# S5 weights stored without the other group's zeros, with one store a tile, two rotation buffers, and the first input transfers issued back to back

## The chip, the cores and the metric

The kernel is one program on one NeuronCore of a Trainium2 chip. Its time is the device time of one execution in microseconds. Five engines run their own instruction streams in order and wait for each other through semaphores: PE (TensorE, matmuls), ACT (ScalarE), DVE (VectorE), POOL (GpSimd) and SP (SyncE, which here only issues transfers). ACT issues transfers too.

## The reference

A sequence of 256 tokens of width 1024 goes through eleven stages: feed-forward blocks and four mixers. Only the first stage (a gated feed-forward block, `ffn0`) and the second (the S5 mixer) are touched. S5 is a linear recurrence in 64 groups with 64 complex states each:

```python
u = h @ w_in                                   # 256 x 1024, 16 channels a group
mag = exp(a_re * dt)
lam_re, lam_im = mag * cos(a_im * dt), mag * sin(a_im * dt)
bb_re, bb_im = cmul(coef_re, coef_im, b_re, b_im)
# for each step t: state = lam * state + bb u_t (complex, by group)
#                  y_t   = Re(c state) + d_skip u_t
g = gelu(y)
g = g * sigmoid(g @ w_glu)
return g @ w_out
```

What depends on the parameters alone (powers of lam, products with b and c) can be worked out before u is there.

## The kernel before

**Order of the work.** The program is recorded as a list of operations with engine, estimated cost and class, and then a list scheduler in the file (`Schedule`) plays it through on its own cost estimates and fixes each engine's order. At run time that order is kept: an instruction that is not ready holds up everything behind it on its engine. Class HEAD goes first, CRIT is the main path, FILL and LATE are weight matmuls, and BACK (the S5 preparation) only takes what the other classes leave. The landing of a transfer is put at `o.lat` = 2.0 us after its issue. All instructions carry the one source line of the emitter, L519, in the profile, so tiles name the work.

**Weights.** Every weight matrix is read in slabs of 512 KB (`raw`), and split into a rounded part by ACT (`whi`) and a rest by DVE (`wlo`); PE multiplies both. Six `raw`, six `whi` and five `wlo` buffers let loads and splits run ahead of PE.

**Head.** `record` puts on ACT's queue, in this order: the gains, the first of eight feature tiles of x (h, k = 0), a one-element activation `tab` that pulls in the activation table, then x's tile 1 and tiles 2 and 3 (`load_x`). Tiles 4 to 7 go on SP's queue between the weights. PE runs ten matmuls on the identity first (`warm`). The first real product needs the split of x's first tile (`xs`) and of the first weight piece.

**S5 preparation** (`s5_prep`, class BACK, during `ffn0`). After small vectors it makes, for the halves of the state dimension (`table(half)`), a table of rotations in the tile `tb` by doubling, and stores it in four pieces. There is one `tb`: the second half starts with two POOL memsets into it, and later `bt` (the b matrix) is loaded into the same tile. Then for each of eight tiles m: `enter(m)` makes `et` from `bt` and a reloaded vector `lb`, four DVE operations and four ACT copies, two for each group mask; `powers(m)` makes `gz`, three DVE operations and two ACT copies; ACT lays b out in `bz`; PE multiplies gz and bz; the product gets d added and is copied by ACT to `lag`. `et` and `gz` hold two groups side by side, and where a row belongs to one group the other group's half is zero. Each of the three goes by its own store from ACT's queue into `s5_dr[m]` (2688 elements a row with the table), from double buffers: `ets[m % 2]`, `gzs[m % 2]`, `lags[m % 2]`.

**S5 stage** (`s5`). `load(m)` reads a whole row block back into `mt` (four buffers, two of them in `ffn0`'s released `hid`; the other two in a pool that opens when all of the preparation has ended, last store included). The profile calls those in the released room `hid`. `state(m)` multiplies `et` with u, DVE runs a chain of products and a scan with the table, `outy(m)` multiplies `gz` and the lags, ACT applies gelu, and `glu(m)` and the projections follow. The first tile waits for `r_bc`, which goes through POOL (`r_col`).

Of the kernel before, what the change touches and what calls it, by code (L numbers as in the profile page):

```python
# [21 lines left out]
P = 128  # L22
T = 256
# [8 lines left out]
MT = 2688  # L32
# [142 lines left out]
class Recorder:  # L175
# [71 lines left out]
    def add(self, calls, cls):  # L247
# [5 lines left out]
        o.lat = 2.0 if o.dma else 0.0  # L253
# [270 lines left out]
class Net:  # L524
# [351 lines left out]
    def s5_prep(self):  # L876
# [9 lines left out]
        self.s5_dn = keep("s5_dn", [P, KD])  # L886
        self.s5_dr = [self.sb(f"s5_dr{m}", [P, MT], pool="dram") for m in range(KD)]
# [111 lines left out]
        tb = tmp("tb", [P, 2, 16, 64])  # L999
# [43 lines left out]
        mask = tmp("mask", [P, 2])  # L1043
        D.dma_start(out=mask, in_=A["s5_mask"])
        bt = tb.rearrange("p r j c -> p (r j c)")[:, 0:1024].rearrange("p (m r c) -> p m r c", m=KD, r=2)
# [9 lines left out]
        for z in gzs + [bz]:  # L1055
            G.memset(z, 0.0)

        def table(half):

            j0 = 16 * half  # L1060
            G.memset(tb[:, 0, :, 31:32], 1.0)
            G.memset(tb[:, 1, :, 31:32], 0.0)
            w = 1
            while w < 32:
                ew = e4[w.bit_length()]
                sh = [P, 2, 16, w]
                a4, b4 = (z[:, 0:32 * w].rearrange("p (r j c) -> p r j c", r=2, j=16) for z in (tA, tB))
                src = tb[:, :, :, 31:31 + w]
                ph = lambda i: ew[:, i, j0:j0 + 16].unsqueeze(1).unsqueeze(3).to_broadcast(sh)
                tt(V, a4, src, ph(0), MUL)  # L1070
                tt(V, b4, src, ph(1), MUL)
                tt(V, tb[:, 0, :, 31 + w:31 + 2 * w], a4[:, 0], b4[:, 1], SUB)
                tt(V, tb[:, 1, :, 31 + w:31 + 2 * w], a4[:, 1], b4[:, 0], ADD)
                w *= 2
            S.activation(tb[:, :, :, 63], e4[6][:, :, j0:j0 + 16], AF.Copy)
            for r in range(2):
                S.activation(tb[:, r, :, 0:31], tb[:, r, :, 62:31:-1], AF.Copy, scale=(1.0, -1.0)[r])
            for m in range(4):
                D.dma_start(out=self.s5_dr[4 * half + m][:, 2176:MT].rearrange("p (r j c) -> p r j c", r=2, j=4),
                            in_=tb[:, :, 4 * m:4 * m + 4, :])  # L1080
# [11 lines left out]
        def enter(m):  # L1092
# [6 lines left out]
            tt(V, a[:, 0], a[:, 0], b[:, 1], SUB)  # L1099
            tt(V, a[:, 1], a[:, 1], b[:, 0], ADD)  # L1100
            et = ets[m % 2]
            for g in range(2):
                for r in range(2):
                    S.activation(et[:, :, r, 64 * g:64 * g + 64], a[:, r], AF.Copy, scale=mask[:, g:g + 1])
            S.dma_start(out=self.s5_dr[m][:, 0:1024], in_=et.rearrange("p s r q -> p (s r q)"))

        def powers(m):
# [4 lines left out]
            gz = gzs[m % 2]  # L1112
# [4 lines left out]
            tt(V, pa, pa, pq, SUB)  # L1117
            for g in range(2):
                ps = slice(64 * g, 64 * g + 64)
                S.activation(gz[ps].rearrange("p r s j (g n) -> p (r s j) g n", g=2)[:, :, g, :],  # L1120
                             pa[ps].rearrange("p q j n -> p (q j) n"), AF.Copy)

        def tile_mats(m):
# [5 lines left out]
            gz = gzs[m % 2]  # L1129
            S.dma_start(out=self.s5_dr[m][:, 1024:2048], in_=gz.rearrange("p r s j q -> p (r s j q)"))  # L1130
            p = self.ps(5)
            with self.r.group(CRIT):
                for ri in range(2):
                    for j in range(4):
                        PE.matmul(p[32 * j:32 * j + 32, 0:P], lhsT=bz[:, ri, j, :], rhs=gz[:, ri, :, j, :], start=(ri == 0), stop=(ri == 1),
                                  skip_group_check=True)
            V.scalar_tensor_tensor(p[:, 0:32], i4, self.s5_dn[:, m:m + 1], p[:, 0:32], op0=MUL, op1=ADD)
            S.activation(lags[m % 2], p[:, 0:P], AF.Copy)
            S.dma_start(out=self.s5_dr[m][:, 2048:2176], in_=lags[m % 2])
# [10 lines left out]
    def s5(self, ph, nxt):  # L1150
# [7 lines left out]
        def share(shape):  # L1158
# [5 lines left out]
            names = "abc"[:len(shape)]  # L1164
# [10 lines left out]
        for t in zss + m4s:  # L1175
            G.memset(t, 0.0)
# [8 lines left out]

        def scale(m):
# [4 lines left out]
        def state(m):  # L1191
            u, mt = us[m], mts[m]
            et = mt[:, 0:1024].rearrange("p (s r q) -> p s r q", s=4, r=2)
            ps = [self.ps(b)[:, 0:P].rearrange("p (r c) -> p r c", r=2) for b in sbanks]
            with self.r.group(CRIT):
                for ri in range(2):
                    for s in range(4):
                        for j in range(4):
                            a = slice(32 * j, 32 * j + 32)
                            PE.matmul(ps[j][:, ri, :], lhsT=et[a, s, ri, :], rhs=u[a, s, :], start=s == 0, stop=s == 3,  # L1200
# [3 lines left out]
            tab = mt[:, 2176:MT].rearrange("p (e j c) -> p e j c", e=2, j=4)  # L1204
# [10 lines left out]
            for ri in range(2):  # L1215
# [3 lines left out]
                            mt[:, 2176:MT].rearrange("p (e q) -> p e q", e=2).unsqueeze(2).to_broadcast([P, 2, 2, T]), op=MUL)  # L1219
# [5 lines left out]
        def outy(m):  # L1225
            z, u, mt = zss[m % NZ], us[m], mts[m]
            gz = mt[:, 1024:2048].rearrange("p (r s j q) -> p r s j q", r=2, s=4, j=4)
            ps = self.ps(4)[:, 0:T].rearrange("p (s c) -> p s c", s=4)
            with self.r.group(CRIT):
                for d in range(4):  # L1230
                    for j in range(4):
                        a = slice(32 * j, 32 * j + 32)
                        PE.matmul(ps[a, d:4, :], lhsT=mt[a, 2048 + 32 * d:2080 + 32 * d], rhs=u[a, 0:4 - d, :], start=d == 0, stop=False,
# [56 lines left out]
        for m in range(KD):  # L1290
            if m < 4:
                umm(m + 4)
            state(m)
# [689 lines left out]
```

## Time and profile before

| | |
|---|---|
| median of 3 runs | 1579.7 us (1579.31 to 1580.79) |
| the profiled execution, its own time | 1576.88 us |
| its span, first to last instruction | 1575.1 us |
| PE busy | 1538.8 us, 98% |
| DVE busy | 1177.5 us, 75% |
| ACT busy | 946.3 us, 60% |

PE is busy nearly all the time, so what the change can move is PE's idle time, the time PE runs at half clock, and PE's own work for the preparation. Times in the trace count from the first instruction; 1.8 us of the execution lie outside the span.

### The profile page before, as it was taken

What the parts mean: (1) busy time and instruction counts of PE and PEld (TensorE: products, weight loads), DVE (VectorE), ACT (ScalarE), POOL (GpSimd) and SP (SyncE); (2) the same over time, 40 slices, a digit from 0 to 9 for tenths busy, and PEclk for the clock granted to TensorE, in tenths of its full rate; (3) what the DMA queues carried; (4) which work ended last, traced back from release to release, by engine and by line L of the source; (5) the groups of instructions that cost most, each with busy time, mean ns of one, the idle gap of its engine ahead of it and who ended that gap; (6) DMA issues with size and microseconds to landing.
All of it is one profiled execution on the core that took longest, in us unless ns stands there. A gap on an engine that the chain in (4) does not pass through costs nothing.

```text
span 1575.1 us, 28813 instructions
## 1 busy us (share of the span) xinstructions
PE 1538.8 (98%) x11018; PEld 1383.7 (88%) x11018; DVE 1177.5 (75%) x2205; ACT 946.3 (60%) x1800; POOL 76.2 (5%) x111
## 2 busy tenths in 40 slices
PE   8998998999999999999999999999999999999998
PEld 8998887998888888889998888989888888888887
DVE  5997878877777777767878777797876557787663
ACT  6566662466655566645666665565787447688642
POOL 1000000000000000003310000010000002100000
PEclk8999999999999999999999999999999999999999
DMA  7667887356656555655447666632665542356561
GB/s 255 216 195 266 255 307 275 133 187 189 187 185 189 184 185 188 187 163 164 134 161 226 188 186 188 207 116 90 217 203 187 188 143 78 122 178 211 186 189 40
DMA packets 94682, 289.29 MB, mean 184 GB/s; under 512 B 18768, under 2 KB 23760, under 8 KB 93520
## 3 DMA queue, kind: packets, MB, share of 16 engines
q1 hardware_dynamic: 90224, 277.44, 55.6%
q10 hardware_dynamic: 4320, 10.01, 1.7%
q8 instruction: 86, 1.41, 0.4%
q14 instruction: 52, 0.43, 0.1%
HBM read 275.22 MB, written 12.19 MB: 182 GB/s over the span
## 4 chain that ended last, share of the span: by engine, by line
PE 86%; DVE 4%; DMA 4%; issue 2%; ACT 2%; POOL 2%; SPq 1%; ACTq 0%; DVEq 0%; POOLq 0%
PE ps L519 86%; DVE wlo L519 1%; DMA s_dr<-tb 1%; DMA raw<-w_s5i 1%; DMA raw<-w_ffn 1%; POOL rs L519 1%; ACT whi L519 1%; SPq L519 1%; DVE h L519 0%; DMA tb<-s_bt 0%; DMA h<-x 0%; DMA tab<-ab_tab 0%; DVE tA L519 0%; POOL qk L519 0%; DMA pb<-s_l 0%
## 5 line engine op out<-in xcount | busy, mean ns | idle before, releaser
L519 ACT ACTIVATE whi<-raw 128x1024 fp32r<-128x1024 f32 (+3 forms) x520 | 522.8, 1011 | 417.4 <-PE ps L519 324.6
L519 PE MATMUL ps<-xs,whi 128*128 128x512 f32 (+1 forms) x2592 | 737.3, 354 | 11.6 <-ACT xs L519 8.4
L519 DVE TENSOR_TENSOR wlo<-raw,whi 128x1024 fp32r<-128x1024 f32 (+3 forms) x520 | 604.4, 1165 | 192.3 <-PE ps L519 145.2
L519 PE MATMUL ps<-xs,wlo 128*128 128x256 f32 x2080 | 567.7, 282 | 0.0
L519 PEld LDWEIGHTS ps<-xs,whi 128*128 128x128 f32 x2592 | 448.5, 190 | 75.6 <-ACT xs L519 9.1
L519 PE MATMUL ps<-hid,whi 128*128 128x512 f32 (+1 forms) x1248 | 424.0, 388 | 0.0
L519 PEld LDWEIGHTS ps<-xs,wlo 128*128 128x128 f32 x2080 | 394.6, 190 | 10.8
L519 PE MATMUL ps<-hid,wlo 128*128 128x256 f32 x1216 | 332.2, 279 | 0.0
L519 PEld LDWEIGHTS ps<-hid,whi 128*128 128x128 f32 x1248 | 229.0, 187 | 49.2 <-issue 0.4
L519 PEld LDWEIGHTS ps<-hid,wlo 128*128 128x128 f32 x1216 | 228.2, 188 | 4.3
L519 PE MATMUL ps<-whi,xs 128*128 128x256 f32 (+1 forms) x544 | 125.6, 312 | 0.0
L519 PEld LDWEIGHTS ps<-whi,xs 128*128 128x128 f32 x544 | 92.1, 188 | 1.0 <-issue 0.8
L519 PE MATMUL ps<-wlo,xs 128*128 128x256 f32 (+1 forms) x272 | 83.3, 306 | 0.0
L519 PE MATMUL ps<-oT,whi 128*128 128x256 f32 x384 | 69.7, 283 | 0.0
L519 POOL TENSOR_TENSOR r_col<-ms,mhalf 128x2 f32<-128x2 f32 x11 | 11.2, 1021 | 1207.2 <-DVE ms L519 1207.2
L519 DVE TENSOR_TENSOR hid<-hv,hid 128x256 fp32r<-128x256 f32 x88 | 37.1, 424 | 31.1 <-ACT hid L519 31.0
L519 PEld LDWEIGHTS ps<-oT,whi 128*128 128x128 f32 x384 | 58.3, 188 | 1.6 <-issue 1.2
L519 ACT ACTIVATE hid<-hv 128x256 fp32r<-128x256 f32 x88 | 36.2, 413 | 33.1 <-DVE hv L519 32.3
L519 ACT ACTIVATE zr<-zr 128x256 f32<-128x256 f32 x128 | 51.0, 410 | 7.4 <-DVE zr L519 7.4
L519 PE MATMUL ps<-oT,wlo 128*128 128x256 f32 x192 | 53.7, 280 | 0.6 <-DVE wlo L519 0.6
L519 PEld LDWEIGHTS ps<-wlo,xs 128*128 128x128 f32 x272 | 51.2, 188 | 0.1
L519 DVE TENSOR_TENSOR zr<-ps,zr 128x256 f32<-128x256 f32 x64 | 26.7, 422 | 28.0 <-ACT zr L519 27.9
(254 smaller groups left out, 1553.4 us busy)
## 6 DMA issues: line engine op xcount, KB each, us to landing
raw<-w_ffn SPq DMA_DIRECT2D x260, 512.0 KB, 4.1
raw<-w_mlp SPq DMA_DIRECT2D x128, 512.0 KB, 4.3
raw<-w_moba_q SPq DMA_DIRECT2D x32, 384.0 KB, 3.0
raw<-w_ab_in SPq DMA_DIRECT2D x18, 512.0 KB, 4.4
hid<-s_dr SPq DMA_DIRECT2D x4, 1344.0 KB, 8.9
mt<-s_dr SPq DMA_DIRECT2D x4, 1344.0 KB, 6.4
s_dr<-gz ACTq DMA_DIRECT2D x8, 512.0 KB, 6.5
s_dr<-et ACTq DMA_DIRECT2D x8, 512.0 KB, 5.8
```

Source lines behind the costliest of these rows:

```text
L519: getattr(getattr(nc, ename), method)(*[real(x) for x in a], **{n: real(x) for n, x in k.items()})
```

## The change

- The preparation keeps `et` and `gz` without the zeros: 512 elements each instead of 1024. With the lags (128) they lie in one tile `outs[m % 2]` of 1152 elements, and one store a tile goes from ACT's queue, after the lags. A row block with the table has 1664 elements instead of 2688.
- The product of gz and bz has 64 columns instead of 128; the group mask goes into two copies to the lags.
- `tb` becomes `tbs`, one tile for each half. `bt` is loaded into the first.
- In the S5 stage a new `spread(m)` puts the zeros back: two masked ACT copies into `ets[m % 2]` and two into `gzs[m % 2]`, before `state(m)`. Their zeros are set once by POOL.
- The scheduler takes 5.0 us instead of 2.0 for the landing of the preparation's transfers.
- The one-element activation between the first transfers goes; the three x transfers of ACT's queue follow each other.

```diff
-MT = 2688
+MT = 1664
...
-        o.lat = 2.0 if o.dma else 0.0
+        o.lat = (5.0 if cls == BACK else 2.0) if o.dma else 0.0
...
-        tb = tmp("tb", [P, 2, 16, 64])
+        tbs = [tmp(f"tb{i}", [P, 2, 16, 64]) for i in range(2)]
...
-        bt = tb.rearrange(...)
+        bt = tbs[0].rearrange(...)
-        gzs = [tmp(f"gz{i}", [P, 2, 4, 4, 32]) for i in range(2)]
-        ets = [tmp(f"et{i}", [P, 4, 2, P]) for i in range(2)]
-        lags = [tmp(f"lag{i}", [P, P]) for i in range(2)]
+        outs = [tmp(f"out{i}", [P, 1152]) for i in range(2)]
...
-        for z in gzs + [bz]:
-            G.memset(z, 0.0)
+        G.tensor_tensor(i4[:, 0:16], i4[:, 0:16], i4[:, 16:32], op=ADD)
+        G.memset(bz, 0.0)
...
+            tb = tbs[half]
             G.memset(tb[:, 0, :, 31:32], 1.0)
...
-            tt(V, a[:, 0], a[:, 0], b[:, 1], SUB)
-            tt(V, a[:, 1], a[:, 1], b[:, 0], ADD)
-            et = ets[m % 2]
-            for g in range(2):
-                for r in range(2):
-                    S.activation(et[:, :, r, 64 * g:64 * g + 64], a[:, r], AF.Copy, scale=mask[:, g:g + 1])
-            S.dma_start(out=self.s5_dr[m][:, 0:1024], in_=et.rearrange("p s r q -> p (s r q)"))
+            e = outs[m % 2][:, 0:512].rearrange("p (r s c) -> p r s c", r=2, s=4)
+            tt(V, e[:, 0], a[:, 0], b[:, 1], SUB)
+            tt(V, e[:, 1], a[:, 1], b[:, 0], ADD)
...
-            tt(V, pa, pa, pq, SUB)
-            for g in range(2):
-                ps = slice(64 * g, 64 * g + 64)
-                S.activation(gz[ps]..., pa[ps]..., AF.Copy)
+            tt(V, outs[m % 2][:, 512:1024].rearrange(...), pa, pq, SUB)
...
-            S.dma_start(out=self.s5_dr[m][:, 1024:2048], in_=gz.rearrange("p r s j q -> p (r s j q)"))
...
-                        PE.matmul(p[32 * j:32 * j + 32, 0:P], lhsT=bz[:, ri, j, :], rhs=gz[:, ri, :, j, :], ...)
+                        PE.matmul(p[32 * j:32 * j + 32, 0:64], lhsT=bz[:, ri, j, :], rhs=gz[:, ri, :, j, :], ...)
...
-            S.activation(lags[m % 2], p[:, 0:P], AF.Copy)
-            S.dma_start(out=self.s5_dr[m][:, 2048:2176], in_=lags[m % 2])
+            for g in range(2):
+                S.activation(o[:, 1024:1152]...[:, :, g, :], p[:, 0:64]..., AF.Copy, scale=mask[:, g:g + 1])
+            S.dma_start(out=self.s5_dr[m][:, 0:1152], in_=o)
...
+        ets, gzs = two("et", (2, 4, P)), two("gz", (2, 4, 4, 32))
-        for t in zss + m4s:
+        for t in zss + m4s + gzs:
             G.memset(t, 0.0)
...
+        def spread(m):
+            mt, et, gz = mts[m], ets[m % 2], gzs[m % 2]
+            for g in range(2):
+                S.activation(et[:, :, :, 64 * g:64 * g + 64]..., mt[:, 0:512]..., AF.Copy, scale=self.s5_mask[:, g:g + 1])
+            for g in range(2):
+                ps = slice(64 * g, 64 * g + 64)
+                S.activation(gz[ps]...[:, :, g, :], mt[ps, 512:1024]..., AF.Copy)
...
+            spread(m)
             state(m)
             outy(m)
...
-            self.load_x(0, 1, "S")
-            self.table(AF.Copy, self.ident)
-            for k in (1, 2):
-                self.load_x(k, 2 * k, "S")
+            for k in (0, 1, 2):
+                self.load_x(k, max(k + 1, 2 * k), "S")
```

## Rows read from the trace of the kernel before

**Rows 1.** Waits of PE, whole span: total us, times, longest us
```profile
PE ps L519 <- ACT xs L519: 8.4, 3, 4.6
PE ps L519 <- ACT gz L519: 6.9, 3, 5.4
```

**Rows 2.** Timeline from 0 to 20 us: start, length, what [idle before, releaser]
```profile
1.36 4.53 PE L519 MATMUL ps<-ident 128*128 128x128 f32 x20 [1.36 <-POOL ones L588]
...
1.66 1.28 ACT L519 ACT_TABLE_LOAD   x1 [1.66 <-PEq L1965]
...
2.96 0.20 ACT L519 ACTIVATE tab<-ident 128x1 f32<-128x1 f32 x1
...
7.87 1.38 ACTq L519 DMA_DIRECT2D h<-x  x2
9.29 0.72 ACT L519 ACTIVATE whi<-raw 128x256 fp32r<-128x256 f32 x2 [6.13 <-DMA raw<-w_ffn]
...
10.46 1.10 PE L519 MATMUL ps<-xs,whi 128*128 128x256 f32 x2 [4.57 <-ACT xs L519]
...
14.40 1.10 PE L519 MATMUL ps<-xs,whi 128*128 128x256 f32 x2 [0.71 <-ACT xs L519]
```

**Rows 3.** Chain that ended last, 0 to 20 us: start, length, what
```profile
3.07 4.78 DMA raw<-w_ffn
...
7.87 5.95 DMA h<-x
```

**Rows 4.** Windows of 1 us on PE: length, busy (count), granted clock, DMA share, GB/s
```profile
18.00:19.00 1.00, 1.00 (x7) 0.50 0.75 303
19.00:20.00 1.00, 1.00 (x9) 0.84 0.75 102
```

**Rows 5.** Chain that ended last, 118 to 150 us
```profile
127.94 7.96 DMA s_dr<-tb
```

**Rows 6.** Waits of DVE, 128 to 228 us
```profile
DVE tA L519 <- POOL tb L519: 6.3, 1, 6.3
...
DVE tA L519 <- DMA tb<-s_bt: 3.2, 1, 3.2
```

**Rows 7.** Windows of 2 us: length, PE, PEld, DVE, ACT, POOL, granted clock, DMA share, GB/s
```profile
146.00:148.00 2.00, 2.00 (x21) 1.58 (x22) 2.00 (x6) 1.66 (x4) 0.00 (x0) 0.50 0.95 166
148.00:150.00 2.00, 2.00 (x15) 2.00 (x15) 1.92 (x6) 0.60 (x2) 0.00 (x0) 0.74 1.01 397
...
226.00:228.00 2.00, 0.44 (x1) 0.29 (x1) 1.76 (x5) 1.58 (x5) 0.00 (x0) 0.88 0.97 346
228.00:230.00 2.00, 2.00 (x10) 1.92 (x10) 0.81 (x3) 1.27 (x3) 0.00 (x0) 0.50 1.02 422
...
234.00:236.00 2.00, 2.00 (x17) 2.00 (x17) 0.31 (x2) 0.39 (x1) 0.00 (x0) 0.91 0.23 95
```

**Rows 8.** Chain that ended last, 196 to 300 us
```profile
225.50 1.14 DVE wlo L519
...
227.56 21.55 PE ps L519 x322
```

**Rows 9.** Timeline of ACT, 219 to 231 us
```profile
228.65 0.33 ACTq L519 DMA_DIRECT2D s_dr<-et  x1
```

**Rows 10.** Timeline of PE, 95 to 160 and 248.5 to 253 us
```profile
99.00 0.64 PE L519 MATMUL ps<-gz,bz 128*32 128x128 f32 x16
...
249.18 2.09 PE L519 MATMUL ps<-hid,mt 32*128 32x64 f32 x64
```

**Rows 11.** Groups of ACT by form, 0 to 240 us: busy, mean ns | idle before
```profile
L519 ACT ACTIVATE gz<-pg 64x512 f32<-64x512 f32 x16 | 10.0, 625 | 0.9 <-DMA s_dr<-tb 0.5 <-DVE pg L519 0.3
```

**Rows 12.** Windows of the preparation and of the S5 stage (columns as rows 7)
```profile
128.00:228.00 100.00, 90.67 (x619) 80.53 (x617) 78.84 (x146) 64.69 (x118) 1.68 (x6) 0.98 0.84 276
237.00:301.00 64.00, 59.01 (x1450) 53.31 (x1451) 55.97 (x109) 16.01 (x29) 0.00 (x0) 0.95 0.59 222
```

**Rows 13.** DMA issues, 100 to 240 us: count, KB each, median us to landing
```profile
s_dr<-gz ACTq DMA_DIRECT2D x7, 512.0 KB, 6.5
```

More of the change, by code (lines that the diff above doesn't have):

```diff
@@ L1078, in table @@
             for m in range(4):
-                D.dma_start(out=self.s5_dr[4 * half + m][:, 2176:MT].rearrange("p (r j c) -> p r j c", r=2, j=4),
+                D.dma_start(out=self.s5_dr[4 * half + m][:, 1152:MT].rearrange("p (r j c) -> p r j c", r=2, j=4),
                             in_=tb[:, :, 4 * m:4 * m + 4, :])
@@ L1116, in powers @@
             tt(V, pq, by(1), rows(0), MUL)
-            tt(V, pa, pa, pq, SUB)
-            for g in range(2):
-                ps = slice(64 * g, 64 * g + 64)
-                S.activation(gz[ps].rearrange("p r s j (g n) -> p (r s j) g n", g=2)[:, :, g, :],
-                             pa[ps].rearrange("p q j n -> p (q j) n"), AF.Copy)
+            tt(V, outs[m % 2][:, 512:1024].rearrange("p (q j n) -> p q j n", q=8, j=4), pa, pq, SUB)
         def tile_mats(m):
@@ L1128, in tile_mats @@
                 S.activation(bz[ps, :, :, g * NN:(g + 1) * NN], bb[ps, :, 4 * m:4 * m + 4, :], AF.Copy)
-            gz = gzs[m % 2]
-            S.dma_start(out=self.s5_dr[m][:, 1024:2048], in_=gz.rearrange("p r s j q -> p (r s j q)"))
+            o = outs[m % 2]
+            gz = o[:, 512:1024].rearrange("p (r s j n) -> p r s j n", r=2, s=4, j=4)
             p = self.ps(5)
@@ L1134, in tile_mats @@
                     for j in range(4):
-                        PE.matmul(p[32 * j:32 * j + 32, 0:P], lhsT=bz[:, ri, j, :], rhs=gz[:, ri, :, j, :], start=(ri == 0), stop=(ri == 1),
+                        PE.matmul(p[32 * j:32 * j + 32, 0:64], lhsT=bz[:, ri, j, :], rhs=gz[:, ri, :, j, :], start=(ri == 0), stop=(ri == 1),
                                   skip_group_check=True)
-            V.scalar_tensor_tensor(p[:, 0:32], i4, self.s5_dn[:, m:m + 1], p[:, 0:32], op0=MUL, op1=ADD)
-            S.activation(lags[m % 2], p[:, 0:P], AF.Copy)
-            S.dma_start(out=self.s5_dr[m][:, 2048:2176], in_=lags[m % 2])
+            V.scalar_tensor_tensor(p[:, 0:16], i4[:, 0:16], self.s5_dn[:, m:m + 1], p[:, 0:16], op0=MUL, op1=ADD)
+            for g in range(2):
+                S.activation(o[:, 1024:1152].rearrange("p (d g n) -> p d g n", d=4, g=2)[:, :, g, :],
+                             p[:, 0:64].rearrange("p (d n) -> p d n", d=4), AF.Copy, scale=mask[:, g:g + 1])
+            S.dma_start(out=self.s5_dr[m][:, 0:1152], in_=o)
         for half in range(2):
@@ L1163, in share @@
             v = room[:, used[0] - n:used[0]].bitcast(F32)
-            names = "abc"[:len(shape)]
+            names = "abde"[:len(shape)]
             return v.rearrange(f"p ({' '.join(names)}) -> p {' '.join(names)}", **dict(zip(names, shape)))
@@ L1199, in state @@
                             a = slice(32 * j, 32 * j + 32)
-                            PE.matmul(ps[j][:, ri, :], lhsT=et[a, s, ri, :], rhs=u[a, s, :], start=s == 0, stop=s == 3,
+                            PE.matmul(ps[j][:, ri, :], lhsT=et[a, ri, s, :], rhs=u[a, s, :], start=s == 0, stop=s == 3,
                                       skip_group_check=True)
@@ L1203, in state @@
             S.activation(m4[:, :, 1:64], self.s5_m4[:, 4 * m:4 * m + 4].unsqueeze(2).to_broadcast([P, 4, 63]), AF.Copy)
-            tab = mt[:, 2176:MT].rearrange("p (e j c) -> p e j c", e=2, j=4)
+            tab = mt[:, 1152:MT].rearrange("p (e j c) -> p e j c", e=2, j=4)
             sh = [P, 2, 2, 64]
@@ L1232, in outy @@
                         a = slice(32 * j, 32 * j + 32)
-                        PE.matmul(ps[a, d:4, :], lhsT=mt[a, 2048 + 32 * d:2080 + 32 * d], rhs=u[a, 0:4 - d, :], start=d == 0, stop=False,
+                        PE.matmul(ps[a, d:4, :], lhsT=mt[a, 1024 + 32 * d:1056 + 32 * d], rhs=u[a, 0:4 - d, :], start=d == 0, stop=False,
                                   skip_group_check=True)
```

15 lines of the change are left out of this document (9 added, 6 removed).

## The prediction

> **What bounds the kernel now.** First the waits of PE over the whole span. PE is the engine that ends last, and its real idle time is small; the three longest single waits lie where this change works. Waits on `xs` come to 8.4 us in three places and waits on `gz` to 6.9 us in three, 5.4 of them in one [rows 1]. The timeline of the head places two waits on `xs`: 4.57 us before 10.46 and 0.71 before 14.40 [rows 2]; what is left of the 8.4, 3.1 us, is the one before 227.56, where S5 begins [rows 8]. Then the windows, for a cost that no idle time shows: after each of the three long waits PE runs at a granted clock of 0.50, that is 1.2 GHz, for some microseconds [rows 4, 7]. The S5 stage itself is crowded: in 64 us PE is busy 59 and DVE 56, but ACT only 16 [rows 12].
>
> So each term is a wait of PE that goes or comes, plus half of the time at half clock behind it.
>
> **Head, term A.** ACT's queue issues x's tiles 1 to 3 only at 7.87, and the chain puts the landing of a weight transfer issued at 3.07 (3.07 + 4.78 = 7.85) right ahead of it [rows 3]. The data of the two have nothing in common. What they can share is the bookkeeping of transfers in program order: with the table load (1.28) and `tab` between them, the x transfers count as later than the weights. ACT's first `whi` stands behind them in its queue and starts at 9.29, PE's first product at 10.46 [rows 2]. With `tab` gone the two issues follow x's tile 0. ACT is free of its first issues by 1.66; the two others take at most 1.38 together, which gives 3.04. The table load is not saved, only moved behind them (1.28, 4.32), and from the first `whi` to the first product it is 10.46 - 9.29 = 1.17, hence 5.49. PE's warm-up matmuls end at 1.36 + 4.53 = 5.89 [rows 2]; they now decide. Should x's tile 0 take the 5.95 of rows 3 from 1.66, the start would be near 8. I take 5.89, since it is issued when few transfers are under way.
>
> The Trainium skill (ScalarE: Activation LUTs, What ACT_TABLE_LOAD costs) speaks against a part of this: a switch costs about 2.66 us, 1.28 for the load and 1.38 for a drain. Here the load takes 1.28 and `tab` starts at 2.96, 0.02 after its end [rows 2]; the trace shows no drain. By the page the first product would come near 6.9 and term A would be about 0.5 us smaller.
>
> Idle time removed: 4.57 + 0.71 = 5.28. The clock is at half until about 19.3 (0.50, then 0.84 in the window 19 to 20 [rows 4]), 8.8 us after the first product. If it rises at that same time, half of the idle time comes back: 2.6. If it rises 8.8 us after the new start, at 14.7: before, by 19.3, PE had done (8.8 - 0.7) / 2 = 4.05 us of full-speed work; after, 4.4 + 4.6 = 9.0, a gain of 4.9. If the warm-up counts, 8.8 us from 1.36 is 10.2, and by 19.3 PE has done 2.2 + 9.1 = 11.3: a gain of 7.2. I take the middle, **-4.9** (-2.1, with the late start, to -7.2).
>
> **Rotation buffers, term B.** The store of the first half's table is issued at 127.94 and lands 7.96 later [rows 5]. The second half's memsets into the same `tb` wait for that on POOL; DVE stands 6.3 us behind them [rows 6], with the operations of `gz` and the weight splits queued behind. ACT's `gz` is late in turn, and PE, in order, stands 5.4 us at a product of gz and bz [rows 1]. Then the clock: 0.50 in 146 to 148, 0.74 in 148 to 150 [rows 7], so 2 + 1.04 us at half, a loss of 1.5. With two tiles the memsets wait for nothing. DVE's next stall, 3.2 us on `bt` loaded into the same tile [rows 6], goes too: the first tile is free once the first half's stores have landed. **-6.9**; with the other waits on gz gone as well (6.9 - 5.4 = 1.5) -8.4; and 0 if another wait takes its place.
>
> **Out buffers, a new wait.** Before, `gz` of six tiles could be made while `et` waited for `bt`. Now both go into `outs[m % 2]`, and tile m + 2 writes there only after the store of m has landed: 6.5 us for the nearest row [rows 13], while the scheduler now counts 5.0. Where it places DVE's write as early as it may, DVE stands some 1.5 us, with `wlo` behind it; five `wlo` buffers hide such a stall, but PE's in-order product of that tile doesn't. Six tiles can wait. Below, nothing; above, one full wait of the kind in term B less its clock, 5.4. I take **+1.5**, the 1.5 of the one short landing.
>
> **S5's start, term C.** PE stops at 227.56 - 3.1 = 224.5; the preparation's last store is issued at 228.65 [rows 9], and its DVE and ACT work stands between the pieces of the last `h` and `xs`; the chain also shows a `wlo` there, 1.14 [rows 8]. PE idles 3.1 us and then runs at half clock: 0.88 in 226 to 228, 0.50 in 228 to 234, 0.91 in 234 to 236 [rows 7], together 6.8 us, a loss of 3.4. If the preparation ends earlier, all of it except the `wlo` can go: 3.1 + 3.4 - 1.1 = 5.4. DVE's work in the preparation stays the same in number and size, and in 128 to 228 it is busy 79 of 100 us [rows 12]. It gets 6.3 + 3.2 = 9.5 us of stall back, but PE comes 6.9 earlier too, so it ends some 3 us earlier against PE, where 228.65 - 224.5 = 4.2 at least would be needed. Half: **-2.7** (0 to -5.4).
>
> **Narrower product, term D.** Eight products of gz and bz stand in PE's queue, 0.64 us for 16 records of 128 columns [rows 10]. The nearest row with 64 columns is S5's `state`, 2.09 us for 64 records, so 0.52 for 16 [rows 10]. 8 x 0.12 = **-1.0**; between nothing and half, -2.6.
>
> The Trainium skill (TensorE: Matmul & The Clock Gate, Wait — 56ns, not 53.3ns?) says that starts of matmuls never come closer than about 25 ns, however few the columns. Rows 10 give 33 ns a record, which agrees. By the page 16 records would take at least 0.40 and the term would end at -1.9.
>
> **The S5 stage, term E.** `spread` puts four ACT copies of 512 columns into each of eight tiles; at 0.625 us for the like [rows 11] that is 2.5 us a tile and 20 us in all. ACT is busy 16 of 64 us there [rows 12], and the loads run ahead of `state`, so the cover is ACT's idle time. If none of it covered, +20. On the other side each row block is 1664 / 2688 = 62% as long in both directions. POOL's memset of the second `gz` waits for the last store of the preparation, and `r_col` stands behind it; with that store issued before PE stops this is hidden. I take **0** (-3 to +10, half uncovered). ACT's work taken out of the preparation (six copies and two stores a tile) was off PE's path. `i4`'s add and the memsets moved out of the head run on POOL, 1.7 us busy in 100 [rows 12]: nothing.
>
> **Sum.** -4.9 - 6.9 + 1.5 - 2.7 - 1.0 + 0 = -14.0 us. The profiled execution took 1576.88, so a profile after would read 1562.9; that execution lies 2.8 us under the median of the runs, so the median goes from 1579.7 to **1565.7**.
>
> **Rivals.**
> - *The head doesn't change*: the x transfers still stand behind weight landings. For it: the trace names no reason for that order. Against: nothing but the table load and `tab` stood between. -9.1: 1570.6.
> - *DVE sets the pace*: in 128 to 228 it has 21 us of idle time [rows 12], and A and B take 12 of PE's time out of the same work; then C gives nothing and a wait of 2 more comes in: -9.3, about 1570.4.
> - *ACT in the S5 stage*: half of `spread` falls in the path, +10: 1575.7. Against it stand the 16 of 64 us.
> - *The ring of two out buffers, slower than before*: a store of the preparation lands late in the way that tb's did, and PE stands at the tile's product 5.4 us and loses 1.5 of clock. One such wait costs 6.9 where I set 1.5; without that 1.5 the gains are 15.5, so from the third of the six possible ones the kernel is slower: 1579.7 - 15.5 + 20.7 = 1584.9. For it: 6.5 against the 5.0 of the scheduler, and every tile passes it. Against: each is short by 1.5 us, not by 6.
> - *More than forecast*: clock early in A, C and D whole, B with both short waits: -7.2 - 8.4 - 5.4 - 2.6 = -23.6, 1556.1.
>
> **How the numbers follow.** Forecast 0.53, head unchanged 0.10, DVE 0.12, ACT 0.10, ring 0.08, more 0.07. No change means within 0.2%, 3.2 us, about what a measurement of this kernel can tell. Slower: 0.08 of the ring and 0.01 of ACT. Same: 0.04 of ACT, 0.03 of the forecast's edge, 0.01 of DVE. The rest is faster, 0.83. The likeliest case alone reaches from 1560 to 1571. The range goes up to 1577, past the centre of the ACT case, and down to 1557: the ring, the upper quarter of ACT, the upper case and a few hundredths of the forecast's edge are left out, 0.2.
>
> **What would show it.** A: in the timeline PE's first product on `xs` near 5.9, x's transfers issued before 3. B: no wait of PE on gz over 1 us near 140, DVE without a wait on POOL's `tb`. C: the wait before S5 under 1.5 us, no window at 0.50 behind it, the last store of the preparation before PE stops. D: products of gz and bz at 0.52. E: the stretch from the first `state` to the last glu no longer than before. The prediction is wrong if PE waits at several products of gz and bz, or on `spread` in S5.

## The result, and the profile after

| | before | after |
|---|---|---|
| median of the runs (4 each, same chip) | 1579.51 us | 1559.38 us |
| ratio, 95% interval | | 0.9874 (0.9857 to 0.9891) |
| profiled execution, its span | 1575.1 us | 1556.6 us |

The kernel is 20.1 us faster; 14.0 were forecast, and 1557 to 1577 was the range. The sum hides that its terms are off on both sides: two of them went another way than forecast, and these partly cancel. Where the two traces part is read from five landmarks on PE, each found in both traces by counting the same instructions:

| landmark on PE | before, us | after, us | gained so far | since the last |
|---|---|---|---|---|
| 64th product on `xs` | 22.89 | 16.84 | 6.05 | 6.05 (head) |
| first down product of `ffn0` | 153.63 | 136.56 | 17.07 | 11.0 (preparation) |
| last down product of `ffn0` | 217.69 | 200.29 | 17.40 | 0.3 |
| first `state` | 236.85 | 221.34 | 15.51 | -1.9 (S5's start) |
| last glu product of S5 | 315.33 | 294.82 | 20.51 | 5.0 (S5 stage) |

Behind that no work is changed. The two profiled executions end 18.5 us apart; the kernel after gives 2 us back near 1010 us, in work that the change doesn't touch (the granted clock is at 0.50 there for 3.4 us, and not in the kernel before). The lines of after that answer to those of before follow.

**Head.** The timeline of the kernel after, 0 to 14 us (start, length, what, [idle before, releaser]), answers to [rows 2]:

```profile
1.17 1.42 ACTq L519 DMA_DIRECT2D h<-x  x3
2.62 1.28 ACT L519 ACT_TABLE_LOAD   x1 [2.62 <-issue]
3.92 0.87 ACT L519 ACTIVATE whi<-raw 128x256 fp32r<-128x256 f32 x2
...
5.24 0.90 PE L519 MATMUL ps<-xs,whi 128*128 128x256 f32 x2
...
10.42 0.38 PE L519 MATMUL ps<-xs,whi 128*128 128x256 f32 x1 [0.37 <-DVE xs L519]
...
13.63 0.39 PE L519 MATMUL ps<-xs,whi 128*128 128x256 f32 x1 [1.54 <-DVE xs L519]
```

The three transfers of x go out one behind the other from 1.17, the table load follows, and the first product starts at 5.24 with no wait, where it had waited 4.57. New waits stand at 10.42 and 13.63. Ahead of the second, the chain shows a weight transfer that is issued at 5.64 and lands 6.17 us later, and then the splits on ACT and DVE: the weights can't keep up with a PE at full speed. It is at full speed: the windows of 1 us on PE (length, busy, granted clock, DMA share, GB/s), which answer to [rows 4], show 1.00 even around the longest of these waits.

```profile
12.00:13.00 1.00, 0.10 (x1) 1.00 1.08 430
...
18.00:19.00 1.00, 1.00 (x11) 1.00 1.00 397
```

**Preparation.** Between 60 and 205 us PE waits for nothing; the 6.9 us on `gz` [rows 1] are gone, and so are DVE's 6.3 and 3.2 us on `tb` [rows 6]. Only two of the eight products of gz and bz now stand ahead of the down products in PE's order, at 94.38 and 99.18; before it was six. Five stand among the down products and the last at 207.00, behind them. Timeline of PE, against [rows 10]:

```profile
94.38 0.43 PE L519 MATMUL ps<-out,bz 128*32 128x64 f32 x16
94.74 0.50 PE L519 MATMUL ps<-xs,whi 128*128 128x256 f32 x2
```

**S5's start.** SP issues the loads of the first two row blocks at 200.71. ACT's timeline, 203 to 222 us, in the place of [rows 9]:

```profile
208.04 0.72 ACT L519 ACTIVATE hid<-hid,s_mask 128x512 f32<-128x512 f32 x1 [3.54 <-DMA hid<-s_dr]
208.67 0.49 ACT L519 ACTIVATE xs<-h,gains 128x256 fp32r<-128x256 f32 x1
...
212.75 0.33 ACTq L519 DMA_DIRECT2D s_dr<-out  x1
218.28 1.33 ACT L519 ACTIVATE et<-hid,s_mask 128x512 f32<-128x512 f32 x2 [5.55 <-DMA s_dr<-out]
...
220.47 0.36 ACT L519 ACTIVATE r_bc<-ps 128x256 f32<-128x256 f32 x1
```

and PE's, 206 to 222 us, in the place of [rows 8]:

```profile
209.21 1.10 PE L519 MATMUL ps<-xs,whi 128*128 128x256 f32 x2 [1.78 <-ACT xs L519]
221.34 0.90 PE L519 MATMUL ps<-hid 32*128 32x64 f32 x24 [2.71 <-DVE hid L519]
```

Read them together. The first masked copy of `spread(0)` stands 3.54 us for the load of the first row block, which takes 7.3 us from its issue, where the scheduler counts 2.0; and the `xs` of the last tile of h is the next instruction on ACT: PE waits 1.78 for it. Then `spread(1)` writes into an `et` of the pool that opens when the last store (issued at 212.75) has landed; ACT stands 5.55 us, `r_bc` is behind it, DVE waits for `r_bc` (5.0 us in the waits of DVE) and PE for DVE, 2.71. One wait of 3.1 has become two of 4.5 together, which is 1.4 of the 1.9 us lost here; the product at 207.00, which before stood ahead of this stretch, is 0.36 more. The clock falls as before [rows 7]:

```profile
210.00:212.00 2.00, 2.00 (x10) 2.00 (x11) 0.96 (x3) 1.96 (x4) 0.00 (x0) 0.50 0.68 268
...
214.00:216.00 2.00, 2.00 (x11) 2.00 (x11) 1.22 (x1) 0.00 (x0) 0.00 (x0) 0.50 0.76 186
```

**S5 stage.** The first 64 us of the stage, from 221 us on, and the transfers' landings (100 to 240 us), against [rows 12, 13]:

```profile
221.00:285.00 64.00, 61.95 (x1486) 56.19 (x1487) 56.53 (x112) 33.28 (x59) 0.00 (x0) 0.97 0.44 149
```
```profile
s_dr<-out ACTq DMA_DIRECT2D x8, 576.0 KB, 5.1
hid<-s_dr SPq DMA_DIRECT2D x4, 832.0 KB, 6.3
```

ACT is busy 33 us where it was 16, as `spread` had to bring, and PE is busier all the same, 62 of 64. In both kernels one part of the stage runs at half clock. Windows of 2 us before, then after (columns as in [rows 7]):

```profile
266.00:268.00 2.00, 2.00 (x47) 2.00 (x44) 0.69 (x2) 0.00 (x0) 0.00 (x0) 0.50 0.96 296
268.00:270.00 2.00, 2.00 (x19) 1.88 (x16) 1.41 (x4) 0.00 (x0) 0.00 (x0) 0.50 0.90 382
```
```profile
222.00:224.00 2.00, 2.00 (x53) 1.88 (x47) 1.85 (x4) 1.37 (x2) 0.00 (x0) 0.75 0.99 402
224.00:226.00 2.00, 2.00 (x11) 2.00 (x10) 1.97 (x6) 1.02 (x2) 0.00 (x0) 0.50 1.03 417
```

With their neighbours these come to 6.8 us at half clock before (264 to 272) and 3.4 after (222 to 228), behind the waits of S5's start. Stores that carry both `et` and `gz` land in 5.1 us, the 5.0 of the scheduler.

### The profile page after: what moved, and what is told of

It reads as the page before. It is cut to its first block, busy times and chain, and to the rows that moved or that the text cites. A ratio compares the mean times of both kernels' runs of the same rounds, so it can differ in the third digit from the quotient of the medians.

```text
span 1556.6 us, 28796 instructions
## 1 busy us (share of the span) xinstructions
PE 1531.4 (98%) x11018; PEld 1377.3 (88%) x11018; DVE 1177.6 (76%) x2205; ACT 946.4 (61%) x1791; POOL 76.7 (5%) x112
## 3 DMA queue, kind: packets, MB, share of 16 engines
q8 instruction: 86, 1.41, 0.4%
## 4 chain that ended last, share of the span: by engine, by line
PE 91%; DVE 4%; DMA 2%; POOL 2%; ACT 1%; issue 1%; SPq 0%; DVEq 0%; POOLq 0%; ACTq 0%
PE ps L519 91%; DVE wlo L519 1%; DVE hid L519 1%; POOL rs L519 1%; DMA hid<-s_dr 0%; DVE h L519 0%; DMA raw<-w_ffn 0%; DMA s_dr<-out 0%; ACT whi L519 0%; DMA raw<-w_mlp 0%; POOL rb L519 0%; POOL qk L519 0%; DVE sa L519 0%; DVE qk L519 0%; DMA gains<-gains 0%
```

## The experiments

Twelve kernels ran, in batches, each batch on one chip together with the kernel before. A gain in us below is one minus the ratio, times the median of the kernel before there (1577 to 1578.5).

### One part alone

**head_only**: the kernel before with the new `record`.

```diff
-            self.load_x(0, 1, "S")
-            self.table(AF.Copy, self.ident)
-            for k in (1, 2):
-                self.load_x(k, 2 * k, "S")
+            for k in (0, 1, 2):
+                self.load_x(k, max(k + 1, 2 * k), "S")
```

> The kernel before with the head's change alone (the one-element activation out, x's transfers issued back to back). My theory: each part's gain stands by itself, and PE is 6.0 us earlier from the 100th product of the first stage on, since the two waits on xs and the half clock go; DVE has enough idle time to follow. So 1573.5, 6 us under the kernel before, and the wait on gz near 140 as long as before, 5.4. Rival, DVE sets the pace of the first stage: the 6 us are eaten by later waits and 2 or less are left, 1577.5 or more.

1571.66 us, ratio 0.9962 (0.9949 to 0.9975): 6.0 gained, all of it by the 64th product (at 16.68). The waits on `gz` stay, 6.6 us in three.

**landing_only**: the kernel before with 5.0 us counted for the landing of the preparation's transfers.

```diff
-        o.lat = 2.0 if o.dma else 0.0
+        o.lat = (5.0 if cls == BACK else 2.0) if o.dma else 0.0
```

> The kernel before with 5.0 instead of 2.0 us for the landing of the preparation's transfers in the scheduler alone. My theory: the first half's store still holds the second half's memsets, but the scheduler now knows it and puts other work ahead, so that the 5.4 us wait on gz shrinks to about 2: 1575 to 1577. Rival: the order hardly changes, 1579 to 1580. Other rival: the scheduler's order for a late landing carries the whole of term B by itself, 1572.5.

1571.08, 0.9960 (0.9943 to 0.9976): 6.3 gained, about twice what was expected and near the other rival's 1572.5. PE's 6.9 us on gz shrink to one wait of 2.3, with one `tb`. In the trace 4.9 us are gained from the 64th product on `xs` to the first down product and 2.7 at S5's start, and the S5 stage gives 2.2 back.

**zeros_only**: the kernel after with one `tb`, the old head (head_only's edit the other way) and 2.0 us: stores without zeros, narrower product and `spread` are what is left.

```diff
-        o.lat = (5.0 if cls == BACK else 2.0) if o.dma else 0.0
+        o.lat = 2.0 if o.dma else 0.0
...
-        tbs = [tmp(f"tb{i}", [P, 2, 16, 64]) for i in range(2)]
+        tbs = [tmp("tb", [P, 2, 16, 64])] * 2
```

> The kernel before with the storage without zeros, one store a tile and spread, but one rotation buffer, 2.0 us for landings in the scheduler and the old head. My theory: what belongs to this part is 1.7 us of narrower products, 5 us of shorter waits in the S5 stage from shorter row blocks, less 1.5 to 3 at S5's start, where spread stands in ACT's queue: 1574 to 1576. Rival, this part carries most of the gain by itself (fewer transfers): 1568 or under. Other rival, spread costs more than the shorter rows give: 1579.5 or over.

1562.28, 0.9913 (0.9889 to 0.9937): 13.7 gained. This fell out far from the expectation, as the first rival had it, and against term B: with one `tb` PE waits for nothing between 30 and 205 us. From the 64th product on `xs` to the first down product it takes 119.72 us. The kernel before takes 130.73 and the kernel after 119.72 as well, so this part alone brings the whole 11.0 of the preparation.

**one_tb**: the kernel after with one `tb`, all else as after (the second line of that diff alone).

> The changed kernel with one rotation buffer for both halves again; all else as changed. My theory: the memsets of the second half wait for the first half's store again, DVE stands 6 us, the preparation ends later and PE stands at a product of gz and bz or at S5's start: 6 to 8 us over the changed kernel, 1565.5 to 1567.5. Rival: with six of the eight products behind the load of bt, PE meets nothing at that place, DVE's stall is covered by the split buffers, and it costs 2 us or less, 1561.5 or under.

1576.48, 0.9992 (0.9977 to 1.0007): 18.6 us slower than after, where 6 to 8 were expected. Not by a wait in the preparation: PE stands nowhere between 14 and 197 us. But the third product stands at 184.78 (154.73 after), and five of the eight at 198.55, 210.24, 230.70, 240.61 and 243.95, past the last down product at 197.52. ACT's timeline:

```profile
202.06 1.05 ACT L519 ACTIVATE whi<-raw 128x1024 fp32r<-128x1024 f32 x1
214.59 1.33 ACT L519 ACTIVATE hid<-hid,s_mask 128x512 f32<-128x512 f32 x2 [11.48 <-DMA hid<-s_dr]
```

`spread(0)` holds ACT 11.48 us. DVE stands 10.62 for the `whi` behind it, and PE 9.88 for DVE. So 13.7 (zeros_only) and 1.3 (this one) differ by the head, which gains, and by the 5.0, which with one `tb` costs: the preparation ends in S5. The likely reason is that the scheduler holds the second half's table until it believes that the first has landed: DVE's doubling for it starts at 129.38 here and at 115.85 in the kernel after.

### Is the second rotation buffer worth anything?

**landing_2us** is the kernel after with 2.0 us again (the first line of zeros_only's diff). **zeros_and_head** has both lines of it and the new head; the two differ by the second buffer alone.

> The kernel after with the one number put back: the scheduler counts 2.0 us again for the landing of the preparation's transfers; two rotation buffers, stores without zeros and the new head stay. By my theory the 5.0 is what makes the preparation late: with it the last store of the kernel after is issued at 212.75, after PE has stopped at 207.4, and spread(1) waits 5.55 us for it. With 2.0 the scheduler puts the last tile some 14 us earlier, the last store goes out before PE stops, and S5 starts 3 to 5 us earlier: 1554 to 1557 us. Rival (the ring): every tile m + 2 is then planned 3 us too early against the landing of the store of m, DVE and PE stand at the products of gz and bz, 1.5 us each at up to six of them, and the time is 1560 to 1566. If neither counts: 1559 within 1.5.

> The kernel after with one rotation buffer instead of two and 2.0 us counted for the landing of the preparation's transfers: what is left of the change is the stores without zeros (with the narrower product and spread) and the new head. Against landing_2us (1557.8) it lacks the second rotation buffer alone. By the prediction's term B the second half's memsets wait again for the first half's store, DVE stands some 6 us at them, and PE stands 5.4 us at a product of gz and bz and runs at half clock behind it: 5 to 7 us slower than landing_2us, 1563 to 1565. Rival: in zeros_only, with one buffer, PE stood at no product; without the zeros' work only two of the eight products stand ahead of the down products in PE's order, and DVE's stall is covered by the buffers of wlo. Then the second buffer is worth nothing here, the parts add up (13.7 and 6.3 of the two single runs), and the time is 1556 to 1559.

landing_2us: 1557.82, 0.9875 (0.9855 to 0.9896). zeros_and_head: 1558.07, 0.9882 (0.9854 to 0.9911). The rival holds: with 2.0 us the second buffer gives nothing that can be measured (the intervals leave some 5 us either way), PE waits at no product for more than 0.2 us, and it is 119.72 us again from the 64th product on `xs` to the first down product. And 13.7 + 6.0 of the single runs is 19.7, the 19.9 of the whole change. DVE's timeline of zeros_and_head shows the same place that stood 6.3 us before [rows 6]:

```profile
117.91 0.21 DVE L519 TENSOR_TENSOR tA<-tb,e 128x32 f32<-128x32 f32 x1 [0.54 <-POOL tb L519]
```

The memsets still wait for the store. But the table's stores land sooner, in a median of 5.2 us here and 8.5 before (90 to 137 us). Here no store of a tile is issued before 152.10; before, five stores of `gz` go out between 98.46 and 134.02. And what DVE still loses reaches no product, since only two stand ahead of the down products. How much of this is the shorter stores and how much the other order wasn't separated.

landing_2us missed its own expectation of 1554 to 1557; the time fits neither effect counting, but in the trace two effects cancel. The last store did go out early, at 201.02, and PE no longer waits at `xs` in S5's start. But the load of the first row block, issued behind two others, landed later, and PE stood at a product in the down phase:

```profile
166.07 1.06 ACT L519 ACTIVATE whi<-raw 128x1024 fp32r<-128x1024 f32 x1 [6.28 <-PE ps L519]
...
168.08 0.42 DVE L519 TENSOR_TENSOR dt<-ps,dt 128x256 f32<-128x256 f32 x1 [5.27 <-ACT dt L519]
...
176.87 0.66 PE L519 MATMUL ps<-out,bz 128*32 128x64 f32 x16 [3.75 <-DVE out L519]
```

This isn't the ring of the rival: no engine waits for a store ahead of that product. ACT's `dt` stands behind a `whi` that waits 6.28 us, DVE waits 5.27 for `dt`, and its `out` comes late.

### S5's start

**spread_later**: 5.0 us instead of 2.0 for S5's loads.

```diff
-            D.dma_start(out=mts[m], in_=self.s5_dr[m])
+            D.dma_start(out=mts[m], in_=self.s5_dr[m]).lat = 5.0
```

> The kernel after, with 5.0 instead of 2.0 us counted for the landing of S5's loads of row blocks alone. In ACT's order spread(0) then stands behind the xs of the last tile of h instead of ahead of it. By my theory of S5's start the wait of 1.78 us before 209.21 goes (ACT stood 3.5 us at spread(0) with that xs behind it), and a part of the half clock behind it (0.50 in 210 to 216): 2 to 4 us faster than the kernel after, 1555 to 1557.5. The wait of 2.71 before the first state stays or grows, since the last store of the preparation comes no earlier in the order. Rival (the wait only moves): PE stops for the same time one step later, at the first state: 1559 within 1.5.

1550.90, 0.9825 (0.9804 to 0.9846): 27.6 us under the kernel before, 7.7 more than the kernel after. It beats both, and by more than expected; the two were measured in different batches, and with both intervals the 7.7 may be 3.5 to 12. Its ACT, then the windows of 2 us on PE:

```profile
204.70 0.51 ACT L519 ACTIVATE xs<-h,gains 128x256 fp32r<-128x256 f32 x1 [0.82 <-DVE h L519]
...
208.59 1.32 ACT L519 ACTIVATE hid<-hid,s_mask 128x512 f32<-128x512 f32 x2
...
212.06 0.36 ACT L519 ACTIVATE r_bc<-ps 128x256 f32<-128x256 f32 x1
...
217.77 1.33 ACT L519 ACTIVATE et<-hid,s_mask 128x512 f32<-128x512 f32 x2 [5.14 <-DMA s_dr<-out]
```
```profile
208.00:210.00 2.00, 2.00 (x18) 1.00 0.99 407
210.00:212.00 2.00, 2.00 (x20) 1.00 0.98 344
```

`xs` runs ahead of `spread(0)`, PE has no gap, and the clock stays at 1.00. `r_bc` has come ahead of `spread(1)` as well, so that ACT's 5.14 us for the last store cost PE only 1.17, one tile later. From the last down product to the first `state` it is 13.3 us; after has 21.1, before 19.2.

**store_first** adds to this that the end of each preparation tile goes into the main path's class:

```diff
+            with self.r.at(CRIT):
+                V.scalar_tensor_tensor(p[:, 0:16], i4[:, 0:16], self.s5_dn[:, m:m + 1], p[:, 0:16], op0=MUL, op1=ADD)
...
+                S.dma_start(out=self.s5_dr[m][:, 0:1152], in_=o).lat = 5.0
```

> The edit of spread_later, and the end of each tile of the preparation (the add of d, the two copies to the lags, and the store) is put into the main path's class, so that the last store isn't put behind the main path's work; in ACT's order r_bc then stands ahead of spread(1). By my theory both waits at S5's start shrink: the 1.78 before 209.21 goes, and the 2.71 before the first state (DVE stood 4.96 at r_bc, which stood behind spread(1), which waited 5.55 for the last store) falls below 1: 4 to 6 us faster than the kernel after, 1553 to 1555.5. Rival (what is hurried pushes the main path back): the DVE and ACT work of the tiles pushes wlo, xs and hid back by as much, eight times some 1 us, and the time is 1559 to 1566.

1560.51, 0.9886 (0.9866 to 0.9906): 18.0, a miss. The time is in the rival's range, but not by its reason: S5's start takes 13.7 us, and the loss lies behind it. The last store came no earlier (213.43), the loads behind it later, and PE stood 3.76 us for one of them, with the clock at 0.50 behind.

**spread_later_3us**: spread_later with 3.0 us for the preparation's transfers.

```diff
-        o.lat = (5.0 if cls == BACK else 2.0) if o.dma else 0.0
+        o.lat = (3.0 if cls == BACK else 2.0) if o.dma else 0.0
```

> The edit of spread_later (5.0 us counted for S5's loads), and 3.0 instead of 5.0 us counted for the landing of the preparation's transfers. In the order that follows, the last store of the preparation stands ahead of the last xs on ACT's queue, and r_bc ahead of spread(1). By my theory the 5.1 us that ACT stands for the last store in spread_later (spread(1), 1.2 us of it on PE) goes, and DVE's 1.6 us at r_bc: 1 to 3 us faster than spread_later, 1548 to 1550 where the kernel before takes 1577.3. Rival (the ring): with 3.0 counted, and 5 to 8 us that the stores take, PE stands at a product of gz and bz in the down products, as in landing_2us (3.8 us there), and the time is 1552 to 1556.

1554.95, 0.9855 (0.9831 to 0.9880): 22.9, worse than spread_later, by neither of the two reasons expected, though inside the ring rival's 1552 to 1556. The last store went out at 202.52. POOL's timeline:

```profile
212.41 0.95 POOL L519 MEMSET gz<- 128x1024 f32 x1 [9.99 <-DMA s_dr<-out]
213.33 0.70 POOL L519 TENSOR_TENSOR r_col<-ms,mhalf 128x2 f32<-128x2 f32 x1
```

The memset of the second `gz` waits for that store until 212.41; `r_col` stands behind it, and PE waited 4.61 for `r_col`. The prediction named this wait under E and put it at nothing if the store is issued before PE stops; here it is, by 7 us, and the wait is there all the same.

### The S5 stage: bytes or order?

**long_loads** and, since that went wrong, **long_loads_in_stage**: eight more transfers of 512 KB, one for each load. The diff is the second's; the first had neither the dependencies nor their order, and read another array.

```diff
-            D.dma_start(out=mts[m], in_=self.s5_dr[m])
+            ld = D.dma_start(out=mts[m], in_=self.s5_dr[m])
+            pad = D.dma_start(out=self.sb(f"s5_pad{m}", [P, 1024], pool="dram"), in_=self.s5_dr[m][:, 0:1024])
...
+            pad.deps.update(d for d in list(ld.deps) + last if d is not ld)
+            pad.lat = 0.0
+            ld.deps.add(pad)
...
```

> The kernel after, and with each of S5's eight loads an extra transfer of 512 KB between two places in memory is issued on the same queue, which nobody waits for; so the stage moves what the kernel before moved (2688 elements a row), while all else is as after. If the S5 stage became shorter because its row blocks are shorter, the stretch from the first state to the last glu product goes from 73.5 us back towards the 78.5 of before, and the median rises by 3 to 5 us to 1562.5 to 1564.5. Rival (the stage gained by another order of its work, not by the bytes): the stretch stays at 73.5 within 1, and the time at 1559.4 within 1.5. Should the first load land later for the extra traffic, that shows ahead of the first state and not in the stretch.

> The edit of long_loads, mended: there the scheduler had issued all eight extra transfers in the head, where nothing held them. Here each extra transfer (512 KB, read from the stored row block and written to another place in memory) is tied to its load and issued directly ahead of it on the same queue, so that the stage moves 2688 elements a row again. If the S5 stage became shorter because its row blocks are shorter, the stretch from the first state to the last glu product goes from 73.5 us to 76 to 79, and the median rises by 3 to 6 us over the kernel after, to 1561 to 1564. Rival (another order of the stage's work, not the bytes): the stretch stays at 73.5 within 1 and what is lost, if anything, is lost ahead of the first state, since the first load lands later: 1557.5 to 1560.5.

long_loads: 1564.03, 0.9916 (0.9897 to 0.9935). It says nothing on the stage: the scheduler issued all eight in the head, 4.5 to 14.7 us, where PE then waited 4.64 and 2.40 us. long_loads_in_stage: 1565.97, 0.9926 (0.9906 to 0.9946), 8 us slower than after, and the stretch from the first `state` to the last glu product takes 83.2 us: 73.5 after, 78.5 before. PE's and DVE's instructions come in the same order as after, so the bytes, or the delay that they bring, lengthen the stage, and not the order. But 83.2 is past the expected 76 to 79 and past the kernel before, so an extra transfer isn't the same as a longer row block, and the run doesn't measure what the shorter blocks alone are worth. What PE does there is odd: it stands 2.49 and 2.00 us in the middle of a block, and the view names no releaser but "issue". Such gaps make up 4.9 us of the stage before and 1.4 after; the timeline of PE before, then after:

```profile
252.88 0.50 PE L519 MATMUL ps<-xs,whi 128*128 128x256 f32 x2 [1.61 <-issue]
...
258.96 3.67 PE L519 MATMUL ps<-hid,mt 32*128 32x64 f32 x128 [1.34 <-issue]
264.61 0.42 PE L519 MATMUL ps<-hid,mt 128*32 128x64 f32 x13 [1.97 <-issue]
```
```profile
242.23 1.55 PE L519 MATMUL ps<-hid,et 32*128 32x64 f32 x43 [0.51 <-issue]
...
256.02 1.05 PE L519 MATMUL ps<-hid 32*32 32x256 f32 x25 [0.93 <-issue]
```

Counted in PE's instructions in the trace (weight loads, matmuls, a drain and some twenty of semaphores), the first one behind each gap is number 4034, 4290 and 4546 before, 4290 and 5058 after: 256 apart, or a multiple of it. The page lists a DMA queue of kind "instruction" with 86 packets, 1.41 MB, so 16 KB each, and PE has 22192 instructions in the trace: 258 a packet.

**shifted_stream** tests that with 128 records more in the head.

```diff
-            self.idle(WARM)
+            for i in range(WARM - 5):
+                self.E["P"].matmul(ps[:, 0:P], lhsT=self.ident, rhs=self.ident, start=True, stop=True)
+            for i in range(37):
+                a = slice(32 * (i % 4), 32 * (i % 4) + 32)
+                self.E["P"].matmul(ps[a, 0:32], lhsT=self.ident[a, a], rhs=self.ident[a, 0:32], start=True, stop=True,
+                                   skip_group_check=True)
...
```

> The kernel after, with five of the ten warm-up matmuls of the head replaced by 37 matmuls of 32 x 32 (their product isn't used): PE's stream gets 128 records (weight loads and matmuls) more ahead of the first product, and the order of all other work is the same on every engine. In the S5 stage PE stands at places where it waits for no semaphore; counted in records of PE from the start, these lie 256 apart: 4034, 4289 and 4545 in the kernel before (1.61, 1.34 and 1.97 us), 4289 and 5057 in the kernel after (0.51 and 0.93), and the same counts in all kernels run so far. Theory: PE's instructions come in pieces of 256 records, and a piece can come late while transfers are in flight. Then the gaps stay at the counts 4033 + 256 k, which are 128 records earlier in the work (half of a state's or an outy's block away from where they were). Rival: the gaps belong to certain instructions of the stage; then they move with the work to counts near 4417 and 5185. The time stays at 1559.4 within 4 in both, since the gaps change in length with the transfers that they meet.

1558.75, 0.9889 (0.9869 to 0.9908), as after. One gap with no releaser is left in the stage, and the instruction behind it is number 5314 = 4034 + 5 x 256: the count holds, the place in the work has moved. The other traces agree: all 22 gaps of 0.5 us or more that the view puts down to "issue" in the stage, in thirteen kernels, lie at 4034 + 256 k. PE's timeline, and the queue in the page:

```profile
259.39 0.58 PE L519 MATMUL ps<-hid 128*32 128x64 f32 x25 [1.20 <-issue]
```
```profile
q8 instruction: 87, 1.43, 0.4%
```

In the trace the last packet of that queue before PE goes on has landed 1.4 to 1.5 us ahead of it: 257.44 for 258.96 and 263.12 for 264.61 before, 240.72 for 242.23 and 254.54 for 256.02 after, 258.03 for 259.39 here. These packets took 0.9 to 1.0 us, as most of the others do; so they weren't slow, but started late, 2.3 to 2.6 us before PE went on. At the other counts of 256 PE ran on.

## Why the prediction came out as it did

**Head, A: -4.9 forecast, -6.0 measured** (head_only, and the same by the landmarks). The mechanism is right in this: x's transfers are issued before 3 us, the table load only moves, and it takes 1.28 as it did. What held them until 7.87 in the kernel before, the bookkeeping of transfers or something else, no run shows. The size is off in two parts. The warm-up matmuls, taken as the bound at 5.89, ended earlier, and the first product starts at 5.24. And the granted clock, for which the middle of three cases was taken, never fell here, where PE no longer stood 4.57 us ahead of its first product; two new waits on `xs`, 1.9 us together, took part of that back. The Trainium skill (ScalarE: Activation LUTs, What ACT_TABLE_LOAD costs) has 1.38 us of drain beside the load; here `whi` starts at 3.92, 0.02 behind the load's end, and the trace again shows none.

**Rotation buffers, B: -6.9 forecast. The size held, the cause did not; that is luck.** PE's waits on gz (6.9) and the half clock behind the long one (1.5) are gone, 8.4, the upper end of the term, and four products moved behind the first down product account for 2.3 more of the 11.0 (four times 0.58, from start to start). But the step "with two tiles the memsets wait for nothing" isn't what did it: zeros_only and zeros_and_head have one tile, no such wait on PE, and the same 119.72 us for the stretch. The storage without zeros did it, with what goes with it (one store a tile, the narrower product, another order). The second buffer only counts together with the 5.0 us: with one buffer and 5.0 the kernel loses 18.6. The prediction priced the 5.0 as a detail of the ring; it moves the time by itself (6.3 in landing_only, on the kernel before; with two buffers and no zeros, 2.0 and 5.0 give the same time within the noise).

**Out buffers: +1.5 forecast, 0 measured** in the kernel after, whose scheduler counts 5.0 where the stores land in 5.1: from 80 to 260 us the only wait for such a store is the 5.55 of `spread(1)`. With 2.0 a product does stand 3.75 us (landing_2us), but behind ACT's `whi` and not for a store.

**S5's start, C: -2.7 forecast, +1.9 measured. This step failed.** It counted DVE's work and took half of the gain for a preparation that ends earlier against PE's stop; the last store is issued at 212.75, 5.3 us behind the end of PE's work at 207.43, and before it was 4.2. The prediction's range for it ended at nothing, because E priced `spread` by its busy time and its cover, and not by what it waits for and who is behind it on ACT's queue. A wait on `spread` in S5, one of the prediction's own signs of being wrong, is what stands there. spread_later shows the mechanism: `xs` and `r_bc` ahead of the waiting copies, and the start takes 13.3 us, 5.9 less than before; the term's best case was 5.4.

**Narrower product, D: -1.0 forecast, -1.7 measured.** Sixteen records take 0.43 instead of 0.64, 0.21 less eight times; the row of `state`, 33 ns a record, was too slow a neighbour. From the start of a block to that of the next work it is 0.36 us, 23 ns a record, with four of these matmuls, which write to different quarters of the output, starting within 20 ns. The Trainium skill (TensorE: Matmul & The Clock Gate, Wait — 56ns, not 53.3ns?) says that starts are never under about 25 ns apart; an estimate from that is 0.40 us for 16, and the measurement is under it.

**S5 stage, E: 0 forecast, -5.0 measured.** That `spread` is covered by ACT's idle time is right within the stage: ACT went from 16 to 33 us of 64 at no cost to PE. The shorter row blocks weren't worth nothing, though: E named them and gave them no price. PE's gaps without a releaser went from 4.9 to 1.4 us, 3.5 less, and the time at half clock, from 6.8 us behind the gap of 1.97 to 3.4 behind S5's start, gives half of the difference, 1.7. Together that is 5.2 for the 5.0. That the gaps shrank because the row blocks are shorter is argued from long_loads_in_stage and not shown by itself.

What stays open: which event asks for an instruction packet, and why one starts late. That it is the traffic of the loads fits long_loads_in_stage and the change of 4.9 to 1.4, but gaps of 1.2 to 2.0 us are also there with the short loads (spread_later, shifted_stream). Nor was it tried to have two rotation buffers in the kernel before.

## What to carry to other kernels

An instruction that waits for a transfer costs what stands behind it on its engine, not its own length: place it by the time at which the transfer really lands. Here that was 7.3 us where the scheduler counted 2.0, and one number in the scheduler was worth 7.7 us. Parts of a change that alter a scheduler's order don't add up; run each alone, and the pairs, before giving one of them the credit. Where PE works through many small matmuls, look for gaps with no releaser and count PE's instructions before you look for a late tile: such a gap keeps its count when the work moves.

## What the hardware showed that was not expected

PE's instructions come over a DMA queue of their own in packets of 16 KB, one for each 256 instructions; in the S5 stage PE stood 0.5 to 2.8 us at some of the packet boundaries. And PE's granted clock stayed at 1.00 through the 1.54 us of waiting near 13 us after, while it was at 0.50 behind the 4.57 us of before, and behind the 1.78 us at 209 after.
